# A delta-rule recurrence by chunks: the triangular matrices by products of their own, both directions in one triangle, operands stored by half stream

## The chip, the cores and the metric

The kernel runs on one core of one Trainium2 chip. The metric is device time in microseconds (us). A core has TensorE (PE, matrix products; its weight loads are shown as PEld), VectorE (DVE), ScalarE (ACT), GpSimd (POOL) and SyncE (SP), which here issues every DMA. Each engine works through its own queue in order and waits on semaphores where it needs what another has made. 

## The reference, cut to what matters

The program is a whole network of three layers over 256 tokens and 256 context tokens of 1024 features, in float32. The change lies in the second layer's mixer, a delta-rule state per head: 16 heads of 64 features, run over the tokens forwards and backwards, first over the context and from its final state over the tokens.

```python
def rwkv7_scan(r, w, k, v, a, b, state, reverse, with_out):
    def step(s, inp):
        rt, wt, kt, vt, at, bt = inp
        sa = jnp.einsum('bhij,bhj->bhi', s, at)
        s = s * wt[:, :, None, :] + sa[..., None] * bt[:, :, None, :] + vt[..., None] * kt[:, :, None, :]
        y = jnp.einsum('bhij,bhj->bhi', s, rt) if with_out else None
        return s, y
...
    yc_f, yc_b, st_f, st_b = bidir(cxt, s0, s0, need_ctx)
    yl_f, yl_b, _, _ = bidir(lat, st_f, st_b, True)
```

The kernel does it by chunks of 32 steps. With a', b', k', r' the operands with their decays, a chunk needs U = (I - tril(a' b'T, -1))^-1 (a' S + tril(a' k'T, -1) V), outputs Y = r' S + tril(r' b'T) U + tril(r' k'T) V, and a new state S. The backward direction has the other triangle.

## The kernel before, in words

**Input stage** (`rwkv_in` and what it starts; about 930 to 1054 us of the profile). Projections and low-rank products run on PE, and for each direction z and each of 8 feature tiles k `ri_item` (L2344) and `ri_decayed` (L2404) make the operands on DVE, ACT and POOL. `ri_send` (L2304) stores each to DRAM: `d_bk` (keys, 512 KB a store), `d_q` (removal keys, 256 KB), `d_rd` (receptances, 128 KB), laid out as [partition, feature tile, time], so that a store writes one run per partition.

**Recurrence** (`rwkv_scan`, L2430; about 1054 to 1357 us). It runs in four units: context first half, context second half, tokens first half, tokens second half (`UNITS`). For a unit j:

- `rw_operands` (L2510) loads, per direction, `we` (two loads of 64 partitions from `d_q`) and `bk` (one load from `d_bk`), and for token units two loads from `d_rd`. A unit is half of the tokens, so a partition's data come in 8 separate runs of 512 bytes (`d_q`, `d_rd`) or 1 KB (`d_bk`).
- `rw_inner` (L2534): 64 items (direction, feature tile, chunk). For each, two products of 64x64 give all four triangles of a chunk (L2551, L2552) in PSUM tile `pA`, two buffers. A mask on DVE (L2558, two per PSUM tile) writes them into `we`, next to the removal keys. POOL then multiplies decays into half of the keys (L2567). Context units take 16 items to a PSUM tile, token units 8, with the receptances beside.
- `rw_items` (L2570) takes the 32x32 blocks to be inverted out of `we`: four transposes of 32 partitions on DVE (L2586), one per direction and parity of the head, into `N`, with reversed axes for the backward direction; after each a POOL memset (L2588) clears the block in `we`.
- `rw_inverse` (L2593): forward substitution, one matrix per partition, all 128 at once: 30 pairs of DVE instructions (L2605, L2607). Two transposes of 64 partitions (L2615) write the inverse to `tt`.
- `rw_chain` (L2712), for two groups of heads: four steps a unit, each a removal product (L2734), a copy, a product with the inverse (L2745), four copies with a scale (L2750), a state product (L2764), two copies (L2775). Token units add outputs (L2797); the last unit a read-out (L2871).

The four inverses run one after the other, and unit j's steps need unit j's inverse.

**The order** is planned in the program: `Weave` (L294) runs all these threads as generators against engines with stated costs, and emits each engine's instructions in the order in which they would start. A cost is only the planner's: it sets places in the queues, not durations. The planner also adds products of no use on PE (`rw_warm`, L2620, into `pX`), which keep TensorE's clock up: where it sees PE idle for more than 0.25 us it fills 80% of the gap, and behind each row of an inverse it adds some where the planned work of PE falls below a share (`DUTY`, 0.5 or 0.55). Those of the second kind wait for their DVE row, and what stands behind them on PE waits too. `rw_heat` (L2630) puts 12 such products ahead of the recurrence, and 8 more that wait for the last load issued so far.

```python
        for k in range(1, 31):
            m = 31 - k
            us = 0.07 + 0.00105 * m * k
...
            row = nc.vector.tensor_tensor(N[:, k + 1 :, :k], N[:, k + 1 :, :k], pr, op=ALU.add)
            self.weave.keep(self.weave.now, 0.0, row)
```

SP's queue at the start holds unit 0's loads (forward, then backward), unit 1's removal keys, then small loads of values `uv` (L2669), each behind a POOL memset of its buffer (L2663), then the rest of unit 1 and unit 2.

Of the kernel before, what the change touches and what calls it, by code (L numbers as in the profile page):

```python
# [18 lines left out]
P = 128  # L19
# [10 lines left out]
class Stream:  # L30
    """A weight matrix as a row of [128, nb] units, loaded in tiles of WCOL
    columns and split into two float32r parts whose sum is exact."""
# [11 lines left out]
    def load(self, t):  # L44
        """a tile of the matrix on its way"""
# [34 lines left out]
class KB:  # L80
# [32 lines left out]
    def open_psum(self, **banks):  # L113
        """all of PSUM: banks per pool"""
# [4 lines left out]
    def open_gemm(self, n=4):  # L119
        """the pools of the products with weights"""  # L120
# [21 lines left out]
    def row_in(self, name, n, pool=None):  # L142
        """a row of n numbers, the same in all partitions"""
# [8 lines left out]
    def act_set(self, after, name):  # L152
        """load a named activation table right behind an instruction"""
# [5 lines left out]
    def mm3(self, ps, wh, wl, xh, xl, start, stop):  # L159
        """ps += (wh + wl).T @ (xh + xl) in three float32r passes"""  # L160
# [9 lines left out]
    def begin(self, g):  # L170
        """runs a generator's first part; the others follow behind later products"""
# [49 lines left out]
    def rstd_tok(self, sums, n, width, scale, eps):  # L221
        """(sums * scale + eps) ** -0.5 on a [128, n] tile"""
# [7 lines left out]
    def sumsq(self, pool, xs, kt):  # L230
        """for each x the sum over its feature tiles of x squared: [128, T], the partitions still to add"""
# [12 lines left out]
    def rstd_from(self, acc, n_feat):  # L244
        """token-major 1/rms [128, 2] from the squares' partial sums"""
# [5 lines left out]
    def bcast_tok(self, rs, pool, col=0, n=2):  # L251
        """rs [128 tokens, n] -> [128, n * 128], the same row in all partitions"""
# [11 lines left out]
class Phase:  # L264
    """pools of one phase: tag -> number of buffers, opened together"""
# [20 lines left out]
def bc(ap, axis, n):  # L286
    """ap with a new axis of n equal entries at free position axis"""
# [6 lines left out]
class Weave:  # L294
    """Emits threads of work, each a generator of requests, in the order in which the
# [1591 lines left out]
class Third(First):  # L1887
# [542 lines left out]
    def rwkv_scan(self):  # L2430
        nc = self.nc
        es = ExitStack()
        with es:
# [707 lines left out]
```

## Time and profile before

| | |
|---|---|
| median of 3 runs | 2858.17 us (2854.01 to 2858.56) |
| profiled execution, span from first to last instruction | 2854.8 us; the page has no other time for this execution |
| input stage of the layer, 930 to 1056 us | DVE busy 110.6 us, PE 109.3 us, DMA engines busy 0.67 of the time |
| recurrence, about 1054 to 1357 us | 303 us, 10.6% of the span |
| of it, from the first product of unit 0 to the last inverse | 1076.6 to 1298.3 us |

A busy share over the whole span says little here, since the network's other layers are products with weights; the recurrence is read by its own stretches.

### The profile page before, as it was taken

The page shows a single profiled execution, that of the slowest core. Times are in us where ns is not written, and L with a number is a line of the kernel's source. Part 1 is how long each engine was busy: PE and PEld are TensorE (multiplying, and loading weights), DVE is VectorE, ACT ScalarE, POOL GpSimd, SP SyncE. Part 2 cuts the span into 40 slices and gives each one's busy share as a digit, 9 for nine tenths or more (in the row PEclk, how much of TensorE's full clock was granted, in tenths as well). Part 3 has the DMA queues.
Part 4 walks back from the last instruction along what each step waited for, and adds up shares of the span by engine and source line. Part 5 has one row for each costly group of instructions (what it writes and reads, how often), then busy time and mean ns, then how long its engine had stood idle before and what let it go on. Part 6 is the DMA issues. An engine that isn't in the chain of part 4 may idle for free.

```text
span 2854.8 us, 52905 instructions
## 1 busy us (share of the span) xinstructions
PE 2654.0 (93%) x22052; PEld 2362.1 (83%) x22052; DVE 1763.1 (62%) x2885; ACT 1297.4 (45%) x2358; POOL 402.5 (14%) x392
## 2 busy tenths in 40 slices
PE   5999999999968879887899999999999999799999
PEld 3977567888757666765899999998999999798999
DVE  4453564334386966885774665776665665765764
ACT  3344333223245541675553544555444444655443
POOL 1210100000044552342100001011001001311100
PEclk9999989999978889998999999999999999999999
DMA  7244735223223675323455455433455554233554
GB/s 274 89 156 152 260 126 191 103 89 104 83 72 107 226 228 114 81 68 96 139 186 179 170 183 198 163 134 119 167 188 177 178 186 172 96 105 110 177 178 148
DMA packets 108142, 426.29 MB, mean 149 GB/s; under 512 B 14334, under 2 KB 50430, under 8 KB 66046
## 3 DMA queue, kind: packets, MB, share of 16 engines
q1 hardware_dynamic: 107326, 420.76, 43.1%
q8 instruction: 173, 2.83, 0.4%
q10 hardware_dynamic: 576, 2.15, 0.2%
q14 instruction: 67, 0.55, 0.1%
HBM read 397.68 MB, written 24.13 MB: 148 GB/s over the span
## 4 chain that ended last, share of the span: by engine, by line
PE 78%; DVE 13%; ACT 4%; POOL 2%; issue 2%; DMA 1%; SPq 0%; ACTq 0%; DVEq 0%; POOLq 0%
PE g L162 20%; PE g L163 20%; PE g L164 20%; PE pG L162 2%; PE pG L163 2%; PE pG L164 2%; DVE pr L2605 2%; DVE N L2607 2%; PE d L1343 2%; PE pX L2623 1%; DVE wl L72 1%; PE pA L2551 1%; POOL acc L495 1%; DVE we L2558 1%; POOL rs L227 1%
## 5 line engine op out<-in xcount | busy, mean ns | idle before, releaser
L72 DVE TENSOR_TENSOR wl<-raw,wh 128x1024 fp32r<-128x1024 f32 x512 | 626.9, 1225 | 427.7 <-ACT wh L71 425.5
L71 ACT CAST wh<-raw 128x1024 fp32r<-128x1024 f32 x512 | 535.2, 1047 | 638.0 <-PE g L163 546.2
L163 PE MATMUL g<-xnl,wh 128*128 128x256 f32 x1504 | 427.9, 285 | 1.0 <-DVE xnl L168 1.0
L162 PE MATMUL g<-xnh,wh 128*128 128x256 f32 x1504 | 427.4, 285 | 1.3 <-ACT xnh L167 1.3
L164 PE MATMUL g<-xnh,wl 128*128 128x256 f32 x1504 | 427.9, 285 | 0.0
L162 PE MATMUL g<-hh,wh 128*128 128x256 f32 (+1 forms) x1216 | 374.4, 308 | 4.9 <-ACT wh L71 3.4
L164 PE MATMUL g<-hh,wl 128*128 128x256 f32 (+1 forms) x1216 | 373.3, 307 | 0.7 <-DVE wl L72 0.7
L163 PE MATMUL g<-hl,wh 128*128 128x256 f32 (+1 forms) x1216 | 373.9, 308 | 0.0
L162 PEld LDWEIGHTS g<-xnh,wh 128*128 128x128 f32 x1504 | 290.5, 193 | 1.7 <-ACT xnh L167 1.7
L163 PEld LDWEIGHTS g<-xnl,wh 128*128 128x128 f32 x1504 | 290.6, 193 | 1.5 <-DVE xnl L168 1.5
L164 PEld LDWEIGHTS g<-xnh,wl 128*128 128x128 f32 x1504 | 290.7, 193 | 0.0
L162 PEld LDWEIGHTS g<-hh,wh 128*128 128x128 f32 x1216 | 234.6, 193 | 17.5 <-ACT wh L71 4.0
L163 PEld LDWEIGHTS g<-hl,wh 128*128 128x128 f32 x1216 | 234.3, 193 | 14.2 <-DVE hl L1382 2.5
L164 PEld LDWEIGHTS g<-hh,wl 128*128 128x128 f32 x1216 | 234.1, 193 | 12.5 <-issue 1.7
L495 POOL TENSOR_TENSOR acc<-acc,sq 128x256 f32<-128x256 f32 x63 | 65.8, 1045 | 863.5 <-ACT sq L494 381.2
L162 PE MATMUL g<-dh,wh 128*128 128x512 f32 (+1 forms) x512 | 172.0, 336 | 0.0
L163 PE MATMUL g<-dl,wh 128*128 128x512 f32 (+1 forms) x512 | 172.0, 336 | 0.0
L164 PE MATMUL g<-dh,wl 128*128 128x512 f32 (+1 forms) x512 | 172.0, 336 | 0.0
L2623 PE MATMUL pX<-ident 128*128 128x256 f32 (+3 forms) x388 | 106.9, 386 | 32.8 <-DVE N L2607 17.9
L163 PE MATMUL g<-wl,hh 128*128 128x256 f32 x448 | 128.4, 287 | 6.9 <-DVE wl L72 6.9
L162 PE MATMUL g<-wh,hh 128*128 128x256 f32 x448 | 131.2, 293 | 3.3 <-ACT wh L71 3.2
L164 PE MATMUL g<-wh,hl 128*128 128x256 f32 x448 | 127.8, 285 | 0.0
(590 smaller groups left out, 5961.7 us busy)
## 6 DMA issues: line engine op xcount, KB each, us to landing
raw<-in_w_mlp SPq DMA_DIRECT2D x64, 1024.0 KB, 4.8
raw<-in_w_ada SPq DMA_DIRECT2D x48, 1024.0 KB, 6.3
raw<-in_w_pre_gu SPq DMA_DIRECT2D x44, 1024.0 KB, 4.8
raw<-in_w_post_gu SPq DMA_DIRECT2D x44, 1024.0 KB, 4.8
raw<-in_w_pre_down SPq DMA_DIRECT2D x22, 1024.0 KB, 4.8
raw<-in_w_post_down SPq DMA_DIRECT2D x22, 1024.0 KB, 4.8
raw<-in_w_ab SPq DMA_DIRECT2D x14, 1024.0 KB, 4.9
d_bk<-h SPq DMA_DIRECT2D x16, 512.0 KB, 3.0
```

Source lines behind the costliest of these rows:

```text
L71: nc.scalar.copy(h[:, :w], r)
L72: nc.vector.tensor_tensor(l[:, :w], r, h[:, :w].bitcast(F32), op=ALU.subtract)
L162: mm(ps, wh, xh, start=start, stop=False)
L163: mm(ps, wh, xl, start=False, stop=False)
L164: mm(ps, wl, xh, start=False, stop=stop)
L227: nc.gpsimd.tensor_tensor(rs[:, :n], ms[:, :n], self.mhalf[:, :n], op=ALU.pow)
L495: nc.gpsimd.tensor_tensor(acc, acc, sq, op=ALU.add)
L1343: nc.tensor.matmul(ps[32 * j : 32 * j + 32], self.cpad[:, k0 + j, 30 - 2 * n : 62 - 2 * n], raw[:, j * 512 : (j + 1) * 512], start=n == 0 ...
L2551: nc.tensor.matmul(ps[64:, i], bk[:64, i0 + i], we[0][:64, :W, i0 + i], start=True, stop=True)
L2605: nc.vector.tensor_tensor(pr, bc(N[:, k + 1 :, k], 2, k), bc(N[:, k, :k], 1, m), op=ALU.mult)
L2607: row = nc.vector.tensor_tensor(N[:, k + 1 :, :k], N[:, k + 1 :, :k], pr, op=ALU.add)
L2623: mm = self.nc.tensor.matmul(o, self.ident, bc(self.ident[:, :64], 1, cols // 64), start=True, stop=True)
```

## The change

- The operands are stored by half stream: `d_bk`, `d_q`, `d_rd` get a leading axis of 4 or 2 halves, so a unit's load reads one run of 4 KB (`we`) or 8 KB (`bk`) per partition, and a store writes 4 (or 2) runs of 512 bytes or 1 KB per partition.
- The backward direction's removal operands are stored in reversed order within a chunk, so that both directions have one triangle; one POOL instruction more per backward tile in `ri_decayed`.
- The matrices to be inverted get products of their own (`rw_matrices`): four of 64x32 per pair of items, two PSUM tiles a unit, each masked by one DVE instruction over 128 partitions into `tt`. One transpose of 128 partitions takes them to `N`, one takes the inverse back.
- `rw_inner` no longer makes that block: products are 64x32, two per item in context units, four in token units; masks of 32 or 64 partitions, two per tile of 16 items in context units, four per tile of 8 in token units. The blocks that were cleared after each transpose are cleared once at the start (12 POOL memsets), ahead of the other POOL work.
- One thread (`rw_products`) orders them: for unit 0 forward inner products, matrices, backward inner products; for the others matrices first. The decays go into the keys after that. The chain waits for all inner products.
- The planner's costs are restated (DVE rows of the inverse 0.2 + 0.0015 m k, ACT copies 0.37, DVE read-out 0.42). `eng = yield "ACT"` still gets ACT, so the copies stay on it.

```diff
-        self.d_bk = [dt(f"d_bk{z}", [P, KT, 2 * 2 * T]) for z in range(2)]
-        self.d_q = [dt(f"d_q{z}", [P, KT, 2 * T]) for z in range(2)]
-        self.d_rd = [dt(f"d_rd{z}", [P, KT, T]) for z in range(2)]
+        self.d_bk = [dt(f"d_bk{z}", [4, P, KT, 2 * T // 2]) for z in range(2)]
+        self.d_q = [dt(f"d_q{z}", [4, P, KT, T // 2]) for z in range(2)]
+        self.d_rd = [dt(f"d_rd{z}", [2, P, KT, T // 2]) for z in range(2)]
...
-        self.nc.sync.dma_start(dst, src)
+        n = dst.shape[0]
+        self.nc.sync.dma_start(dst.rearrange("b p f -> p b f"), src.rearrange("p (b f) -> p b f", b=n))
...
-        kp, bp = bk[:, :, z], bk[:, :, 1 - z]
+        kp, bp = bk[:, :, z], rv3(bk[:, :, 1 - z])
...
+            self.on(eng).tensor_tensor(co[:, :, :, :0:-1], ck[:, :, :, :31], cE[:, :, :, 1:], op=ALU.mult)
+            yield "Pool", 0.1
+            nc.gpsimd.tensor_tensor(o[:, :, 0], kk[:, :, 31], E[:, :, 32], op=ALU.mult)
+            yield "Pool", 0.1
+            nc.gpsimd.tensor_copy(o[:, :, 32], kk[:, :, 63])
...
+            for j, u in enumerate(self.us):
+                for z in range(2):
+                    for par in range(2):
+                        r = self.row(par, 1 - z)
+                        nc.gpsimd.memset(u["we"][par][r : r + 32, 0, z * 32 : z * 32 + 32], 0.0)
...
+    def rw_products(self):
+        for j, (s, h) in enumerate(self.UNITS):
+            if j > 0:
+                yield from self.rw_matrices(j)
+            yield from self.rw_inner(j, s, 0)
+            if j == 0:
+                yield from self.rw_matrices(j)
+                yield from self.rw_keys_end(j, 0)
+            yield from self.rw_inner(j, s, 1)
...
-                    yield "PE", 0.64, 0.0 if i + 4 < per else 0.15, 0.17 * W
-                nc.tensor.matmul(ps[64:, i], bk[:64, i0 + i], we[0][:64, :W, i0 + i], start=True, stop=True)
-                nc.tensor.matmul(ps[:64, i], bk[64:, i0 + i], we[1][64:, :W, i0 + i], start=True, stop=True)
+                    yield "PE", 0.32 * W, 0.0 if i + 4 < per else 0.15, 0.17 * W
+                for second in (z, 1 - z)[:W]:
+                    for par in range(2):
+                        r, o = slice(64 * par, 64 * par + 64), self.row(par, second)
+                        w = slice(0, W) if second == z else slice(1, W)
+                        nc.tensor.matmul(ps[o : o + 32, i, w], bk[r, i0 + i, 32 * second : 32 * second + 32], we[par][r, w, i0 + i], start=True, stop=True)
...
+    def rw_matrices(self, j):
...
+        for i0 in range(0, 32, 16):
+            a = yield "take", "A"
+            ps = self.pA[a].rearrange("p (i t) -> p i t", t=32)
+            for i in range(16):
+                if i % 4 == 0:
+                    yield "PE", 0.64, 0.0 if i + 4 < 16 else 0.15, 0.17
+                for z in range(2):
+                    for par in range(2):
+                        q, r = 2 * z + par, slice(64 * par, 64 * par + 64)
+                        it = z * 32 + i0 + i
+                        nc.tensor.matmul(ps[32 * q : 32 * q + 32, i], bk[r, it, 32 * (1 - z) : 32 * (1 - z) + 32], we[par][r, 0, it], start=True, stop=True)
+            yield "DVE", 0.6
+            nc.vector.tensor_tensor(u["tt"][:, i0 : i0 + 16], ps, bc(self.nmask, 1, 16), op=ALU.mult)
...
-                yield "DVE", 1.13
-                rows = we[par][r0 : r0 + 32, 0, z * 32 : z * 32 + 32]
-                nc.vector.transpose(Nq[:, ::-1, ::-1] if z else Nq, rows.rearrange("p i t -> p t i"))
-                yield "Pool", 0.9
-                nc.gpsimd.memset(rows, 0.0)
+        yield "wait", ("matrices", j)
+        yield "DVE", 1.94
+        nc.vector.transpose(N, self.unit(j)["tt"].rearrange("p i t -> p t i"))
...
-            us = 0.07 + 0.00105 * m * k
+            us = 0.2 + 0.0015 * m * k
...
-        for z in range(2):
-            r = slice(64 * z, 64 * z + 64)
-            yield "DVE", 1.13
-            row = nc.vector.transpose(tt[r].rearrange("p i t -> p t i"), N[r, ::-1, ::-1] if z else N[r])
+        yield "DVE", 1.94
+        row = nc.vector.transpose(tt.rearrange("p i t -> p t i"), N)
```

## Rows read from the trace of the kernel before

**Rows 1.** The page: span, and the chain that ended last by line.
```profile
span 2854.8 us, 52905 instructions
PE g L162 20%; PE g L163 20%; PE g L164 20%; PE pG L162 2%; PE pG L163 2%; PE pG L164 2%; DVE pr L2605 2%; DVE N L2607 2%; PE d L1343 2%; PE pX L2623 1%; DVE wl L72 1%; PE pA L2551 1%; POOL acc L495 1%; DVE we L2558 1%; POOL rs L227 1%
```
**Rows 2.** Busy time by stretch: window, its length, engines with counts, clock, DMA share, GB/s.
```profile
930.00:1056.00 126.00, 109.30 (x607) 84.15 (x606) 110.56 (x130) 69.34 (x108) 74.85 (x79) 0.89 0.67 228
1060.00:1076.00 16.00, 8.86 (x28) 7.01 (x27) 0.00 (x0) 0.00 (x0) 0.00 (x0) 0.68 1.01 227
1136.40:1186.80 50.40, 44.37 (x1068) 36.87 (x1056) 45.33 (x82) 35.60 (x88) 13.25 (x20) 0.95 0.17 43
1186.80:1241.40 54.60, 48.24 (x1109) 39.73 (x1108) 45.53 (x82) 33.84 (x84) 21.09 (x28) 0.94 0.38 92
1241.40:1298.30 56.90, 43.68 (x1112) 35.90 (x1112) 51.16 (x70) 35.82 (x91) 29.21 (x32) 0.86 0.31 71
1298.30:1357.00 58.70, 45.78 (x1208) 36.12 (x1207) 28.64 (x74) 36.52 (x88) 14.25 (x15) 0.95 0.34 109
```
**Rows 3.** Groups of instructions from 1136.4 to 1298.3 us, units 1 to 3.
```profile
L2623 PE MATMUL pX<-ident 128*128 128x64 f32 (+3 forms) x183 | 44.4, 345 | 19.3 <-DVE N L2607 14.2 <-DVE tt L2615 5.0
...
L2558 DVE TENSOR_TENSOR we<-pA,amask 64x512 f32<-64x512 f32 x36 | 24.6, 688 | 13.3 <-PE pA L2552 12.4
```
**Rows 4.** PE in order of time, up to the first inner product.
```profile
1070.11 6.58 PE L2623 MATMUL pX<-ident 128*128 128x256 f32 x16 [7.14 <-DMA we<-d_q]
1076.62 0.24 PE L2551 MATMUL pA<-we,bk 64*64 64x32 f32 x1
```
**Rows 5.** DVE in order of time, around the first inverse.
```profile
1091.78 1.41 DVE L2558 TENSOR_TENSOR we<-pA,amask 64x512 f32<-64x512 f32 x2 [5.89 <-PE pA L2552]
1093.21 1.94 DVE L2586 STREAM_TRANSPOSE N<-we 32x1024 f32<-32x1024 f32 x1
...
1105.44 1.94 DVE L2586 STREAM_TRANSPOSE N<-we 32x1024 f32<-32x1024 f32 x1
1107.42 0.20 DVE L2605 TENSOR_TENSOR pr<-N 128x30 f32<-128x30 f32 x1
...
1132.49 3.90 DVE L2615 STREAM_TRANSPOSE tt<-N 64x1024 f32<-64x1024 f32 x2
```
**Rows 6.** Groups of instructions in the whole recurrence, shapes apart.
```profile
L2586 DVE STREAM_TRANSPOSE N<-we 32x1024 f32<-32x1024 f32 x16 | 31.0, 1939 | 0.5
L2615 DVE STREAM_TRANSPOSE tt<-N 64x1024 f32<-64x1024 f32 x8 | 15.4, 1924 | 0.2
L2588 POOL MEMSET we<- 32x1024 f32 x16 | 15.1, 944 | 47.8 <-DVE N L2586 44.4 <-PE pU L2745 2.4 <-DMA we<-d_q 0.9
L2879 DVE TENSOR_TENSOR we<-pY,we 128x256 f32<-128x256 f32 x8 | 3.3, 417 | 11.9 <-PE pY L2797 11.9
```
**Rows 7.** PE in order of time: products among the first inner products, and the first chain step.
```profile
1081.95 0.70 PE L2623 MATMUL pX<-ident 128*128 128x256 f32 x2
1082.58 0.24 PE L2551 MATMUL pA<-we,bk 64*64 64x32 f32 x1
1083.16 0.70 PE L2623 MATMUL pX<-ident 128*128 128x256 f32 x2
...
1137.15 0.65 PE L2745 MATMUL pU<-wsb,tt 32*32 32x64 f32 x32
1137.73 0.92 PE L2623 MATMUL pX<-ident 128*128 128x256 f32 x4
```
**Rows 8.** DMA issues: KB each, us from issue to landing (page; recurrence; input stage).
```profile
raw<-in_w_mlp SPq DMA_DIRECT2D x64, 1024.0 KB, 4.8
...
bk<-d_bk SPq DMA_DIRECT2D x6, 1024.0 KB, 9.0
we<-d_q SPq DMA_DIRECT2D x12, 256.0 KB, 9.7
...
d_bk<-h SPq DMA_DIRECT2D x16, 512.0 KB, 3.0
```

More of the change, by code (lines that the diff above doesn't have):

```diff
@@ L2568, in rw_inner @@
             yield "set", ("keys", j, z, q)
+    def rw_matrices(self, j):
+        nc = self.nc
+        u = self.unit(j)
+        we, bk = u["we"], u["bk"]
+        for z in range(2):
+            yield "wait", ("operands", j, z)
+        for i0 in range(0, 32, 16):
[4 more added lines that the diff above has]
+                    yield "PE", 0.64, 0.0 if i + 4 < 16 else 0.15, 0.17
+                for z in range(2):
+                    for par in range(2):
+                        q, r = 2 * z + par, slice(64 * par, 64 * par + 64)
[3 more added lines that the diff above has]
+            nc.vector.tensor_tensor(u["tt"][:, i0 : i0 + 16], ps, bc(self.nmask, 1, 16), op=ALU.mult)
+            yield "give", ("A", a)
+        yield "set", ("matrices", j)
     def rw_items(self, j):
         nc = self.nc
[L2573 removed]
+        N = self.Ns[j % 2]
         if j > 1:
             yield "wait", ("inv", j - 2)
[L2576 to L2588 removed]
+        yield "wait", ("matrices", j)
+        yield "DVE", 1.94
+        nc.vector.transpose(N, self.unit(j)["tt"].rearrange("p i t -> p t i"))
         yield "Pool", 0.15
@@ L2608, in rw_inverse @@
             self.weave.keep(self.weave.now, 0.0, row)
-        if j > 2:
-            for g in range(2):
-                yield "wait", ("chain", j - 3, g)
-        for z in range(2):
-            r = slice(64 * z, 64 * z + 64)
-            yield "DVE", 1.13
-            row = nc.vector.transpose(tt[r].rearrange("p i t -> p t i"), N[r, ::-1, ::-1] if z else N[r])
-            if z == 0:
-                self.weave.keep(self.weave.now, 0.0, row)
+        yield "DVE", 1.94
+        row = nc.vector.transpose(tt.rearrange("p i t -> p t i"), N)
+        self.weave.keep(self.weave.now, 0.0, row)
         yield "set", ("inv", j)
@@ L2638, in rw_heat, with copy @@
                 self.rw_warm(256, after)
+    def copy(self, eng, o, i):
+        (self.nc.scalar.copy if eng == "ACT" else self.nc.vector.tensor_copy)(o, i)
     def chunk(self, z, i):
@@ L2718, in rw_chain @@
             yield "wait", ("inv", j)
+            per = 16 // (2 - s)
+            for end in range(per, 65, per):
+                yield "wait", ("inner", j, end)
             self.weave.DUTY = self.DUTIES[1 + (j == len(self.UNITS) - 1)]
@@ L2744, in rw_chain @@
                             u0 = self.row(par, 1 - z)
-                            nc.tensor.matmul(pu[u0 : u0 + 32, z, k], tt[r, item(0, k) if z == 0 else item(1, k) - 32], w[r, k * 64 : k * 64 + 64], start=True, stop=True)
+                            nc.tensor.matmul(pu[u0 : u0 + 32, z, k], tt[r, item(z, k) - 32 * z], w[r, k * 64 : k * 64 + 64], start=True, stop=True)
                 for z in range(2):
@@ L2801, in rw_output @@
             return
-        yield "ACT", 0.27
+        yield "ACT", 0.37
         nc.scalar.copy(ys, yp)
@@ L2868, in rw_pools @@
             self.wo.fill(KT)
-            yield "DVE", 1.13
+            yield "DVE", 1.94
     def rw_readout(self, g, m, yp):
@@ L2906, in rw_readout @@
         pv = pt.rearrange("p k (z t) -> p k z t", z=2)
-        yield "ACT", 0.27
+        yield "ACT", 0.37
         nc.scalar.copy(at(self.ch), pv)
-        yield "DVE", 0.35
+        yield "DVE", 0.42
         nc.vector.tensor_tensor(at(self.cl), pv, at(self.ch).bitcast(F32), op=ALU.subtract)
```

104 lines of the change are left out of this document (59 added, 45 removed).

## The prediction

> **What bounds the kernel now.** I read the page first: most of the chain that ended last is weight products of other layers; the recurrence shows as inverse rows (L2605, L2607), products of no use (L2623), inner products and masks [rows 1]. So the change can only act in about 303 us, and there the busy time by stretch decides. From the end of the first inverse to the end of the last, 1136.4 to 1298.3 us, DVE is busy 45.33 + 45.53 + 51.16 = 142.0 of 161.9 us, PE 44.37 + 48.24 + 43.68 = 136.3, ACT less; behind it, without inverses, DVE needs half of its time [rows 2]. The groups of that stretch then say who waits for whom: PE's products of no use stood idle for 19.3 us, for DVE rows 14.2 and for the transposes back 5.0 [rows 3]. DVE sets the pace there, with PE close behind. The view in order of time shows the head: PE waits 7.14 us for a load of removal keys, spends 6.58 us on the eight products tied to it, and starts inner products at 1076.62 [rows 4]; the first inverse starts at 1107.42, 30.8 us later, behind masks and four transposes, and runs 25.1 us plus 3.9 us of transposes [rows 5].
>
> **The change, step by step.** The sum stands against the span of 2854.8 us [rows 1]; the median of the runs is 3.4 us above it, and I apply the difference to the median, 2858.2.
>
> 1. *Stores in shorter runs.* 16 stores each of 512, 256 and 128 KB (14.7 MB) are cut to runs of 512 bytes and 1 KB. The input stage moves 228 GB/s at a DMA share of 0.67, some 340 GB/s when all engines work; loads in runs of that short length gave 227 GB/s at a share of 1.01 [rows 2]. So the stores take about 65 us of all engines in place of 43, and the share rises to some 0.85 of 126 us. They lie beside DVE, busy 110.6 of 126 us [rows 2]; the cover is thinner, and a buffer may come free late. SP's issue of a store in four runs costs more, beside that work too. The extra POOL instruction on each of 8 backward tiles is small and shares POOL's slack (74.85 of 126 us busy). I take +2 us: bounds 0 (all hidden) and +6 (a quarter of the 22 us shows). A gain is excluded: nothing here gets shorter.
> 2. *Loads in longer runs.* A 1 MB load of `bk` lands after 9.0 us, one of 256 KB in the same queue after 9.7, a 1 MB weight load in long runs after 4.8 [rows 8]. PE waits 7.14 us for such a load [rows 4]. I take -4: bounds 0 and -7.1, the whole wait. The 12 memsets of 0.944 us [rows 6], 11.3 us, stand ahead of the `uv` memsets on POOL, so the small loads of `uv` and what is behind them on SP (unit 1's keys) may wait a few us; unit 1 is not needed until the first inverse runs. I cost that at nothing; without that cover it is at most 11.3 us of unit 1's start.
> 3. *From the first inner product to the first inverse.* Today PE takes four items of inner products and two products of no use every 1.21 us, 0.63 of it the latter [rows 7]; 16 such groups stand ahead of the last mask, then transposes [rows 5]. Afterwards 8 groups of forward inner products, whose planned PE time is halved (I take 0.8 us: 0.58 and some filler), then 8 groups of matrices. Such a group has 16 products, 32 records; 32 records of 32x32 took 0.58 us [rows 7], with filler 1.21. 8 x 0.8 + 8 x 1.21 = 16.1, one mask 0.69, one transpose 1.94 (32 and 64 partitions cost the same, 1.94 and 1.92 [rows 6], so 128 should), waits 1: 20 us in place of 30.8, -11. Bounds: -8 (all groups at 1.21) and -19 (no filler). The row gives 18 ns a record.
>    The Trainium skill (TensorE: Matmul & The Clock Gate, "Wait — 56ns, not 53.3ns?") says that matmuls never start less than about 25 ns apart however small they are. By that a group of matrices would take 0.8 us, an estimate, and step 3 would be -9; the row shows 18 ns, and the row decides.
> 4. *The first inverse.* One transpose back instead of two: -1.9. But other DVE work now stands among its rows: four backward masks (2.75), unit 1's two matrix masks (1.4), its transpose (1.94) and, as PE delivers them, four of its masks (2.75): +8.8. Net +7. Bounds +1 (only the backward masks) and +12.
> 5. *Units 1 to 3, DVE.* Transposes out: 12 of 1.94 become 2 (unit 1's is in step 4), -19.4. Transposes back: 6 of 1.92 become 3, -5.8. Masks: 36 of 0.688 (24.8 [rows 3]) become 4 of unit 1, 4 of matrices, and 64 of 256 columns, for which the nearest row is 0.417 [rows 6]: 2.8 + 2.8 + 26.7 = 32.3, +7.5. Net -17.7 of 142.0, and with the idle 19.9 us kept, 144 in place of 161.9. The 16 POOL memsets [rows 6] leave too; no engine but POOL and its own successors waited on them, so nothing.
> 6. *The same stretch, PE.* Matrices of units 2 and 3: 16 groups of 0.58 us, +9.3; token units' inner products go from two to four per item, but a group of four items then has 32 records, 0.58 us by the 32x32 row, where a group of 16 larger ones took 0.58 in a context unit [rows 7] (I take the same for token units): +2, for what a change of shape may cost. PE's list becomes about 148 us with 44.4 us of filler in it [rows 2, 3]; of its 25.6 idle us, 19.3 are waits for DVE that shrink. So PE allows no better than 148 to 154. I take 148, -14: between DVE's 144 and PE's 154, nearer to DVE, since real products displace some filler. Bounds -28 (idle halved too, filler down) and 0.
> 7. *The last unit* (58.7 us [rows 2]): its chain is untouched, 0.
>
> Sum: +2 - 4 - 11 + 7 - 14 = -20, so 2838 us.
>
> **The rivals.** *DVE stays filled and filler gives way* (gain larger): half of the 19.9 idle us vanish and PE drops as much filler; step 6 becomes -28 and the sum -34, 2824 us. For it: waits for PE by masks (12.4 us [rows 3]) shrink when products come earlier. Against: PE's list.
> *PE becomes the bound*: step 6 is -4 rather than -14, the sum -10, 2848 us. For it: PE is busy 136.3 of 161.9 already [rows 2]. The Trainium skill's 25 ns of step 3, if it held for these products, would lead here: 48 groups of 32 records in the stretch at 0.8 us in place of 0.58, +10.6, an estimate; the row speaks against it.
> *Slower, by the planner's own filler.* The restated costs make a planned inverse 26.9 us of row time instead of 14.6 (the sums of both formulas over 30 pairs); the rows really took 25.1 [rows 5]. PE gaps in the plan are filled, and a planned stretch that is 12.3 us longer per inverse may be filled to 80%: 3 x 9.8 = 29.5 us more products in PE's own queue, which no engine can skip. PE's list is then 148 + 29.5 = 177.5, +15.6 on the stretch in place of -14: the sum is +9.6, 2868 us. It decides from the point where filler in the stretch exceeds the 44.4 us of now by about 20. For it: PE's queue is in order. Against: the same longer plan ends the waits of PE for rows (14.2 us), and masks that the plan now sets among the rows use up planned time.
> *The change gives nothing* (within 6 us): loads gain nothing, since the weight load's 4.8 us was measured with nothing else in its queue, and steps 4 and 6 eat step 3. Around 2857.
>    Of the loads, the Trainium skill (DMA: Bandwidth & Descriptors, Specifications) puts the least transfer for full rate at 512 bytes. By it neither the shorter stores nor the longer loads change a rate, steps 1 and 2 are 0 and the sum is -18; the row with 227 GB/s at full share speaks against it [rows 2].
>
> **How the numbers follow.** The forecast (2828 to 2844) gets 0.50, the larger gain 0.20, PE as the bound 0.13, nothing 0.09, slower 0.08. About 0.2%, 5.7 us, is what a measurement of this kernel can tell from no change: faster 0.83, same 0.09, slower 0.08. The range takes in the forecast, most of the larger gain and PE as the bound with the ends of steps 1 to 4: 2815 to 2854.
>
> **What would show it.** Right: the first L2605 row some 15 us sooner after the input stage than now, one transpose of about 1.94 us on each side of every inverse, DVE busy near 125 us between the first and last inverse, that stretch near 148 us, the last stage unchanged. Step 2: the wait of PE for a load under 4 us. Step 1 is wrong if the input stage ends over 6 us later. The forecast is wrong if a transpose of 128 partitions costs more than 1.94, if masks of 256 columns cost 0.688 as those of 512 (then +17 us on DVE, and the gain is gone), or if the products of no use exceed 44.4 us by 20 in the stretch.

## The result and the profile after

The changed kernel takes **2885.8 us** (median of 4 runs, 2883.4 to 2886.9), where the kernel before took 2856.1 beside it: ratio 1.0102, 95% interval 1.0088 to 1.0116. It is 29 us slower by the ratio; the forecast was 20 us faster, and the range ended at 2854. The page of the changed kernel, span and chain that ended last by line (compare [rows 1]):

```profile
span 2885.1 us, 56428 instructions
PE g L162 19%; PE g L163 19%; PE g L164 19%; PE pX L2675 3%; PE pG L162 2%; PE pG L163 2%; PE pG L164 2%; PE d L1343 2%; PE pS L2826 1%; DVE wl L72 1%; POOL acc L495 1%; DVE N L2665 1%; PE pA L2589 1%; POOL rs L227 1%; DVE pr L2663 1%
```

Products of no use (L2675, before L2623) rise from 1% to 3% of the chain, and the inverse's rows fall from 4% to 2%. The chain has moved from DVE's rows to PE's products. The busy time by stretch says where (columns as in [rows 2]):

```profile
930.00:1058.00 128.00, 113.25 (x609) 87.78 (x608) 110.95 (x130) 70.24 (x108) 75.28 (x81) 0.86 0.71 227
1130.00:1160.50 30.50, 28.24 (x664) 23.01 (x668) 28.28 (x63) 22.66 (x56) 7.84 (x11) 1.00 0.09 24
1160.50:1206.70 46.20, 41.61 (x1078) 33.55 (x1072) 8.08 (x10) 26.66 (x67) 9.21 (x14) 0.93 0.42 111
1206.70:1252.50 45.80, 39.91 (x1054) 31.37 (x1041) 38.48 (x93) 17.89 (x43) 11.26 (x15) 0.96 0.36 76
1252.50:1277.20 24.70, 24.34 (x780) 19.61 (x783) 3.31 (x3) 19.25 (x51) 22.16 (x23) 1.00 0.11 26
1277.20:1323.40 46.20, 42.29 (x1116) 33.36 (x1109) 39.14 (x94) 18.84 (x47) 12.06 (x17) 0.93 0.26 82
1323.40:1388.00 64.60, 54.84 (x1232) 45.45 (x1233) 32.16 (x83) 38.31 (x96) 11.07 (x12) 0.97 0.20 62
```

Inverses are called here by their unit: first inverse for unit 0, then inverse 1, 2 and 3, which is the last. The first inverse ends at 1130.0, 6.4 us sooner than in [rows 2]. From there to the end of the last one 193.4 us pass, against 161.9. DVE does less (28.28 + 8.08 + 38.48 + 3.31 + 39.14 = 117.3 us, against 142.0), so its idle time goes from 19.9 to 76.1 us. Nearly all of the growth lies in the third and the fifth line: 46.2 us with 8.1 us of DVE work, 24.7 with 3.3. DVE in order of time shows the first hole, from the end of inverse 1 to the start of inverse 2:

```profile
1158.52 1.95 DVE L2668 STREAM_TRANSPOSE tt<-N 128x1024 f32<-128x1024 f32 x1
1160.50 2.00 DVE L2598 TENSOR_TENSOR we<-pA,amask 32x512 f32<-32x512 f32 x3
1171.18 1.41 DVE L2598 TENSOR_TENSOR we<-pA,amask 32x512 f32<-32x512 f32 x2 [8.68 <-PE pA L2589]
1174.85 1.41 DVE L2598 TENSOR_TENSOR we<-pA,amask 32x512 f32<-32x512 f32 x2 [2.26 <-PE pA L2589]
1191.60 0.69 DVE L2634 TENSOR_TENSOR tt<-pA,nmask 128x512 f32<-128x512 f32 x1 [15.35 <-PE pA L2632]
1203.96 0.69 DVE L2634 TENSOR_TENSOR tt<-pA,nmask 128x512 f32<-128x512 f32 x1 [11.67 <-PE pA L2632]
1204.69 1.97 DVE L2646 STREAM_TRANSPOSE N<-tt 128x1024 f32<-128x1024 f32 x1
```

Read it upwards. Inverse 2 waits for the masks of unit 2's matrices (L2634), these for PE's products (L2632, 15.35 and 11.67 us). The matrices stand in `rw_products` behind unit 1's inner products, whose last masks (L2598) run at 1160 to 1176, behind inverse 1. In the kernel before, with the same lag on unit 1's masks (`MASK`), they could not slide so far: the blocks to be inverted came out of those masks, so inverse 1's transposes waited for them. DVE there, behind the first inverse:

```profile
1136.42 2.60 DVE L2558 TENSOR_TENSOR we<-pA,amask 64x512 f32<-64x512 f32 x4
1139.05 1.93 DVE L2586 STREAM_TRANSPOSE N<-we 32x1024 f32<-32x1024 f32 x1
```

After the change inverse 1 asks for unit 1's matrices alone, and seven of unit 1's eight masks run behind it. What PE does in that hole, its groups from 1160.5 to 1204.7 us:

```profile
L2675 PE MATMUL pX<-ident 128*128 128x256 f32 (+3 forms) x68 | 17.2, 359 | 0.0
L2826 PE MATMUL pS<-uv,bki 128*64 128x64 f32 x192 | 7.7, 240 | 0.2 <-ACT uv L2693 0.2
...
L2632 PE MATMUL pA<-we,bk 64*32 64x32 f32 x256 | 4.5, 207 | 3.3 <-issue 3.3
```

A count behind x is of the profile's records, and a product of this kernel leaves two of them: the 20 products of `rw_heat` are 40 records. Below, products of no use are counted in records; the x2 of [rows 7] is one product, where the prediction says two.

4.5 us of matrices share the hole with 17.2 us of products of no use and six state products of the chain. In the second hole, from inverse 2's end to the start of inverse 3, PE is busy 22.43 of 22.80 us, 8.9 of them with products of no use (the stretch, with PE, clock, DMA share and GB/s, and one of its groups):

```profile
1252.50:1275.30 22.80, 22.43 (x700) 1.00 0.09 22
L2675 PE MATMUL pX<-ident 128*128 128x256 f32 (+2 forms) x36 | 8.9, 342 | 0.0
```

In the whole stretch from 1130.0 to 1323.4 us the products of no use take 82.5 us, where [rows 3] has 44.4:

```profile
L2675 PE MATMUL pX<-ident 128*128 128x256 f32 (+3 forms) x334 | 82.5, 360 | 9.8 <-DVE N L2665 8.3 <-DVE tt L2668 1.2
```

The last stage is nearly as before: from the end of the last inverse to the end of the read-out (1384.5, before 1357.7) 61.1 us, before 59.4.

### The profile page after: what moved, and what is told of

Same layout as the page of the kernel before. It is cut to its first block, busy times and chain, and to the rows that moved or that the text cites. A ratio compares the mean times of both kernels' runs of the same rounds, so it can differ in the third digit from the quotient of the medians.

```text
span 2885.1 us, 56428 instructions
## 1 busy us (share of the span) xinstructions
PE 2698.6 (94%) x23794; PEld 2402.9 (83%) x23794; DVE 1732.0 (60%) x2909; ACT 1297.2 (45%) x2358; POOL 402.5 (14%) x396
## 4 chain that ended last, share of the span: by engine, by line
PE 79%; DVE 10%; ACT 4%; issue 2%; POOL 2%; DMA 1%; SPq 0%; ACTq 0%; DVEq 0%; POOLq 0%
PE g L162 19%; PE g L163 19%; PE g L164 19%; PE pX L2675 3%; PE pG L162 2%; PE pG L163 2%; PE pG L164 2%; PE d L1343 2%; PE pS L2826 1%; DVE wl L72 1%; POOL acc L495 1%; DVE N L2665 1%; PE pA L2589 1%; POOL rs L227 1%; DVE pr L2663 1%
## 5 line engine op out<-in xcount | busy, mean ns | idle before, releaser
L2675 PE MATMUL pX<-ident 128*128 128x256 f32 (+3 forms) x594 | 148.3, 373 | 18.1 <-DVE N L2665 10.3
L2675 PEld LDWEIGHTS pX<-ident 128*128 128x128 f32 x594 | 102.8, 203 | 38.5 <-DVE N L2665 15.0
```

Source lines behind the costliest of these rows:

```text
L2675: mm = self.nc.tensor.matmul(o, self.ident, bc(self.ident[:, :64], 1, cols // 64), start=True, stop=True)
```

## The experiments

**Theories.** A: unit 1's masks let rows go first (`MASK`, 0.2 us for unit 1) and hold both PSUM tiles `pA` meanwhile, so unit 2's matrices, next in the thread, come only after inverse 1. B: products of no use make PE late. C: the restated costs spoil the planned order. D: the storage costs the time. The expectations call the products that the duty asks for "tied to rows"; more exactly, duty 0 takes away those behind a row and those that the planner puts ahead of a product where the planned share falls short, and leaves those that fill gaps.

**The storage alone, on the kernel before (e1).**

```diff
-        self.d_bk = [dt(f"d_bk{z}", [P, KT, 2 * 2 * T]) for z in range(2)]
+        self.d_bk = [dt(f"d_bk{z}", [4, P, KT, 2 * T // 2]) for z in range(2)]
...
-        load(u["bk"][:, it], self.d_bk[z][:, :, 2 * tk.start : 2 * tk.stop])
+        load(u["bk"][:, it], self.d_bk[z][2 * s + b])
```

(and `d_q`, `d_rd`, `ri_send` as in the change.)

> The kernel before with the storage by half stream alone (stores in 2 or 4 runs per partition, loads in one run). Steps 1 and 2 of the prediction together are -2 us, so about 2854 us. Theory A (the products' order makes inverses 2 and 3 start late): 2850 to 2860 us, first inner product within 4 us of 1076.6. A rival that puts the loss into the input stage and the loads (short stores, contention): 2870 us or more, the input stage ending over 6 us later.

Measured: 0.9994 of before (0.9981 to 1.0007). D falls. The first inner product was not within 4 us of 1076.6 in the profiled execution, the slowest of its ten (2864.8 us): it started at 1081.4, behind a longer wait for a load than before (7.14 in [rows 4]):

```profile
1074.86 6.63 PE L2624 MATMUL pX<-ident 128*128 128x256 f32 x16 [9.39 <-DMA we<-d_q]
```

**Masks at once (e2).**

```diff
-    MASK = 0.0, 0.2, 0.0, 0.0
+    MASK = 0.0, 0.0, 0.0, 0.0
```

> The changed kernel, but unit 1's masks no longer let the inverse's rows go first (lag 0 in place of 0.2 us). Theory A (the masks of unit 1 hold both PSUM tiles of the products, so unit 2's matrices, behind them in the same thread, come after inverse 1): unit 2's matrices are done before inverse 1 ends, inverse 2 begins under 8 us behind inverse 1 in place of 46 us, and the time falls by 15 to 40 us, to 2845 to 2870 us, even though masks now stand among inverse 1's rows. Theory B (the planner's products of no use lengthen PE's queue): their number stays near 600, so 2880 to 2890 us. Theory C (the restated costs): no change, 2880 to 2890 us.

Measured: 1.0032 of before (1.0012 to 1.0052), so 20 us under the changed kernel's 1.0102, with 530 records of products of no use in place of 594. DVE in order of time, at the place of the hole:

```profile
1182.88 1.94 DVE L2668 STREAM_TRANSPOSE tt<-N 128x1024 f32<-128x1024 f32 x1
1184.85 1.73 DVE L2598 TENSOR_TENSOR we<-pA,amask 32x256 f32<-32x256 f32 x4
1186.50 1.97 DVE L2646 STREAM_TRANSPOSE N<-tt 128x1024 f32<-128x1024 f32 x1
```

Inverse 2 begins 1.7 us behind inverse 1, its matrices being masked from 1137.9 on, before inverse 1 began. The masks now lie among the rows: the first inverse ends at 1142.2, 12 us later than in the changed kernel, 3.3 of it because the first inner product started later in this execution. The second hole shrinks too, from 22.8 to 8.9 us. A holds.

**No products of no use (e3), and the same on the kernel before (e5).**

```diff
-            w.BIAS, w.AGING = 0.02, 0.1
+            w.BIAS, w.AGING, w.FILL = 0.02, 0.1, 0.0
...
-    DUTIES = 0.5, 0.55, 0.5
+    DUTIES = 0.0, 0.0, 0.0
```

> The changed kernel without the products of no use in the recurrence (duty 0 and gaps left open; the 20 of heat ahead of it stay). Theory B: the idle stretches of DVE of 46 and 25 us between the inverses shrink to under 15 us each, and the time falls to 2840 to 2860 us, unless the granted clock falls to its lower level for most of the recurrence. Theory A: unit 2's matrices still come only behind unit 1's masks, so inverse 2 still begins 30 us or more behind inverse 1; the time moves by less than 12 us at the same clock, 2874 to 2895 us.

> The kernel before without the products of no use in the recurrence (duty 0, gaps left open; the 20 of heat stay): the control to the same edit on the changed kernel, which took 25 us off it. Theory B' (products of no use cost the changed kernel time that they do not cost the kernel before, since only there PE stands in the way of the next unit's matrices): before moves by less than 12 us, 2846 to 2870 us. Rival (products of no use cost any version of this recurrence some 25 us): 2828 to 2840 us.

Measured: e3 1.0015 of before (1.0001 to 1.0028), 25 us under the changed kernel, though the granted clock was 0.61 up to the end of the first inverse. The hole ahead of inverse 2 is still 29 us (1154.4 to 1183.7), as A says; the one ahead of inverse 3 is gone (1.1 us), as B says. Neither expectation alone was right. e5: 1.0038 (1.0022 to 1.0054), 11 us slower: there the products of no use are worth their place. The granted clock was 0.57 from 1060 to 1140 us, close to the lower of its two levels (1.2 of 2.4 GHz), with PE busy 38.25 of 80 us:

```profile
1060.00:1140.00 80.00, 38.25 (x614) 33.48 (x612) 48.11 (x85) 6.61 (x18) 20.65 (x26) 0.57 0.60 135
```

**The old costs (e4), and the new costs on the kernel before (e9).**

```diff
-            us = 0.2 + 0.0015 * m * k
+            us = 0.07 + 0.00105 * m * k
...
-                        eng = yield "ACT", 0.37, 0.0
+                        eng = yield "ACT", 0.27, 0.0
```

(and so at each of the other restated lines; e9 is the reverse.)

> The changed kernel with the planner's costs of before (rows of an inverse 0.07 + 0.00105 m k, ACT copies 0.27, DVE read-out 0.35); no instruction is other, only the order and the number of the products of no use. Theory C: the loss goes, 2835 to 2860 us. Theory A: the lag of unit 1's masks stays, inverse 2 begins 25 us or more behind inverse 1, and the time falls by no more than 12 us, 2874 to 2888 us. Theory B: the planned inverse is 12 us shorter each, so 100 or more fewer products of no use and 2850 to 2870 us.

> The kernel before with the restated costs of the planner alone (rows of an inverse 0.2 + 0.0015 m k, ACT copies 0.37, DVE read-out 0.42): the prediction's third rival taken by itself. That rival, with its terms: some 30 us more of products of no use in the stretch, +15 to +25 us, 2870 to 2885 us. Theory A with B (the loss needs the new products' thread, in whose way the filler stands): more filler, but the next unit's triangles come with its inner products early, so within 10 us of before, 2850 to 2868 us.

Measured: e4 1.0113 (1.0097 to 1.0129), no gain; inverse 2 begins 46.6 us behind inverse 1, and 544 records of products of no use are left, so B's way to a gain did not open. In e4's stretch between first and last inverse (1128.7 to 1327.8 us) they take as long as in the changed kernel, with the old costs:

```profile
L2675 PE MATMUL pX<-ident 128*128 128x64 f32 (+3 forms) x322 | 82.1, 364 | 14.0 <-DVE N L2665 12.5 <-issue 0.8 <-DVE tt L2668 0.3
```

So the restated costs are not what makes the changed kernel slow, and C falls. e9: 1.0046 (1.0031 to 1.0060), 13 us slower, between the two expected effects (15 to 25, and under 10); products of no use in the stretch between first and last inverse rise from 44.4 [rows 3] to 63.0 us, and the stretch from 161.9 to 174.4 us. So the prediction's third rival exists on the kernel before, at about half of its price.

**Both edits (e6).** The diffs of e2 and e3 together:

```diff
-            w.BIAS, w.AGING = 0.02, 0.1
+            w.BIAS, w.AGING, w.FILL = 0.02, 0.1, 0.0
...
-    DUTIES = 0.5, 0.55, 0.5
+    DUTIES = 0.0, 0.0, 0.0
...
-    MASK = 0.0, 0.2, 0.0, 0.0
+    MASK = 0.0, 0.0, 0.0, 0.0
```

> The changed kernel with unit 1's masks at once (lag 0) and without products of no use: both edits together. If they act on two different waits (A on the order of the products' thread, B on the length of PE's queue), their gains of 20 and 25 us add up: 2835 to 2850 us, with no idle of DVE over 10 us between inverses. If they are two ways to the same place (unit 2's matrices come sooner), no more than the larger: 2855 to 2870 us.

Measured: **0.9927 of before (0.9898 to 0.9956)**, 2841.8 us: better than both kernels, and 44 us under the changed one by the medians, 50 by the ratios, so the gains of 20 and 25 add up. Stretches up to the end of the first inverse, to that of the last, and behind it:

```profile
1060.00:1139.80 79.80, 41.34 (x1396) 35.34 (x1395) 40.22 (x85) 6.61 (x18) 31.34 (x41) 0.65 0.53 141
1139.80:1284.70 144.90, 102.89 (x3836) 85.04 (x3836) 119.97 (x253) 105.38 (x262) 52.86 (x68) 0.92 0.30 78
1284.70:1345.00 60.30, 38.98 (x1124) 32.80 (x1124) 28.78 (x74) 36.47 (x86) 14.75 (x16) 0.75 0.33 105
```

144.9 us between first and last inverse with DVE busy 120.0: the forecast had 148 and about 125.

**Which products of no use cost (e10, e13, e14).** Duty 0 with gaps still filled, with masks at once (e10) and without (e13); and gaps open with the duty kept (e14):

```diff
-    DUTIES = 0.5, 0.55, 0.5
+    DUTIES = 0.0, 0.0, 0.0
```

e10 has this and the diff of e2, e13 this alone, and e14:

```diff
-            w.BIAS, w.AGING = 0.02, 0.1
+            w.BIAS, w.AGING, w.FILL = 0.02, 0.1, 0.0
```

> The changed kernel with masks at once and duty 0, but gaps in PE's plan filled as in the kernels before and after (so only the products that wait for a row of an inverse are gone). If it is the products tied to rows that cost time in the changed kernel: as without any, 2835 to 2848 us, or 3 to 8 us better by a granted clock near 0.96 in place of 0.61 to 0.95. If any product of no use in PE's queue costs: between 2850 and 2868 us.

> The changed kernel without the products of no use that are tied to rows (duty 0), gaps filled as before, lag of unit 1's masks kept. If the tied kind costs the 25 us by the order that it makes: 2855 to 2868 us, as without any. If it is the mere time of products of no use in PE's queue: their gap kind still costs, 2870 to 2885 us.

> The changed kernel without the products that fill gaps, those tied to rows kept; the planned order is that of the changed kernel. If the tied kind and its order cost the 25 us: within 6 us of the changed kernel, 2880 to 2892 us. If the time of the gap kind in PE's queue costs: 2862 to 2876 us.

Measured: e10 0.9935 (0.9910 to 0.9960), e13 1.0013 (0.9999 to 1.0028): each as the run without any (e6, e3), though e10 has 260 and e13 288 records of these products against 40. What fills a gap of PE costs nothing that these runs can tell (the intervals of e13 and e3 leave room for some 5 us, those of e10 and e6 for some 10), and the clock that it gives back (0.76 in place of 0.65 up to the first inverse's end in e10) gains nothing that can be measured. e14: 1.0102 (1.0079 to 1.0124), as the changed kernel. It tells less than was meant, since the duty asks for most of what the gaps had (570 records are left of 594). So it is the duty that costs 25 us (e13 against the changed kernel). PE's groups in the same hole of e13, 1158.5 to 1189.9 us:

```profile
L2675 PE MATMUL pX<-ident 128*128 128x256 f32 (+3 forms) x28 | 7.4, 393 | 0.0
L2826 PE MATMUL pS<-uv,bki 128*64 128x64 f32 x114 | 5.0, 250 | 0.2 <-ACT uv L2693 0.2
...
L2632 PE MATMUL pA<-we,bk 64*32 64x32 f32 x256 | 3.5, 212 | 0.0
```

The hole is 31.4 us in place of 44.2: 9.8 us less of products of no use and 78 records less of state products stand between the same 256 records of the matrices. In neither hole do products of no use wait for anything (idle 0.0), and no inverse runs there, so here it is their place ahead of the matrices that costs, not a row that they are tied to. The second hole goes from 22.8 to 1.1 us with the duty, but inverses 2 and 3 take longer (53 and 50 us from transpose to transpose, 44 each in the changed kernel): the stretch between first and last inverse is 173.7 us in e13, 193.4 in the changed kernel.

**The restated costs without the duty (e15, and its control e16).** On the kernel before, duty 0 with gaps filled; e15 has the new costs too:

```diff
-    DUTIES = 0.5, 0.55, 0.5
+    DUTIES = 0.0, 0.0, 0.0
```

And in e15 alone, with the other restated lines:

```diff
-            us = 0.07 + 0.00105 * m * k
+            us = 0.2 + 0.0015 * m * k
```

> The kernel before with the restated costs and without the tied kind. If the restated costs act through the tied kind (a longer planned inverse asks for more of it): the 13 us that they cost alone are gone, no slower than the kernel before with the tied kind left out (e16), within 6 us. If they act by the places that they give to rows and masks: 10 us or more slower than e16.

> The kernel before without the tied kind, gaps filled: the control to e15, and to the 11 us that leaving out both kinds costs the kernel before. If that loss comes from the lower granted clock (0.57 ahead of the first inverse): filled gaps give it back, 2856 to 2866 us. If it comes from the order that is planned without the tied kind: 2868 to 2878 us again.

Measured: e16 1.0025 (1.0010 to 1.0040), e15 0.9969 (0.9954 to 0.9984). The same costs that lose 13 us with the duty gain 16 without it. On the kernel before they cost time through the duty, then, and apart from that they make the better plan. e16 is 4 us under e5, within both intervals; its filled gaps raised the granted clock up to the first inverse's end only from 0.57 to 0.64, so how much of e5's loss is the clock and how much the order stays open.

**Other versions (e7, e8, e11, e12, e17, e18).** All have masks at once. e8 and e17 give the matrices of units 1 to 3 a thread of their own, and take them out of `rw_products`:

```diff
             w.add(self.rw_products(), 1)
+            w.add(self.rw_mats(), 1)
...
+    def rw_mats(self):
+        yield "wait", ("matrices", 0)
+        for j in range(1, len(self.UNITS)):
+            yield from self.rw_matrices(j)
```

They and e18 have duty 0 and gaps open, as e6; e8 and e18 have the costs of e4. e7 has the costs of e4, filled gaps and a duty of 0.3:

```diff
-    DUTIES = 0.5, 0.55, 0.5
+    DUTIES = 0.3, 0.3, 0.3
```

e11 and e12 have gaps open and a duty of 0.2, and e12 the old cost of rows and a lower one of matrices:

```diff
-    DUTIES = 0.5, 0.55, 0.5
+    DUTIES = 0.2, 0.2, 0.2
...
-                    yield "PE", 0.64, 0.0 if i + 4 < 16 else 0.15, 0.17
+                    yield "PE", 0.4, 0.0 if i + 4 < 16 else 0.15, 0.17
...
-            us = 0.2 + 0.0015 * m * k
+            us = 0.07 + 0.00105 * m * k
```

> The changed kernel with unit 1's masks at once, the planner's costs of before and a duty of 0.3 in place of 0.5 and 0.55 (fewer products of no use, gaps still filled). By A and B together: unit 2's matrices before inverse 1 ends, under 350 products of no use, 2825 to 2850 us. If the restated costs matter beside them (C, in part), it is under 2835 us; if old costs only make the order worse, as alone, 2855 to 2875 us.

> The changed kernel with the matrices of units 1 to 3 in a thread of their own, so that they no longer stand behind a unit's inner products, unit 1's masks at once, old costs, no products of no use. Theory A, if the one thread matters beside the lag: the matrices of units 2 and 3 are done before the inverse ahead ends, DVE is idle under 5 us between inverses, 2820 to 2845 us. If the lag alone mattered: as the same without the thread, within 6 us of 2845 us.

> The same with duty 0.2 and no filled gaps: fewer than 100 products of no use. If the lower clock in the first inverse (0.61 without filler) costs what the longer first inverse suggests, 5 to 10 us come back: 2830 to 2838 us. If not, 2836 to 2848 us, as without any.

> The changed kernel with masks at once, duty 0.2, no filled gaps, the cost of the rows alone as before (0.07 + 0.00105 m k) and the matrices' products planned at 0.4 us a group of four in place of 0.64, near what the trace shows (0.39). If what is left is the order of the products against the rows (masks among the rows of the first inverses, unit 3's matrices late): under 2835 us, inverses 1 to 3 within 140 us of the first one's end. If the rows' restated cost is the better one: 2840 to 2860 us.

> As e6 (masks at once, no products of no use, restated costs), with the matrices of units 1 to 3 in a thread of their own. If the one thread costs something beside the lag: 2825 to 2838 us, under e6. If it was the thread that made e8 slow: 2850 to 2866 us. If neither: within 6 us of e6, 2836 to 2848 us.

> As e6, with the costs of before in place of the restated ones, one thread. If the old costs made e8 slow: 2855 to 2868 us. If they do not matter without tied products: within 6 us of e6, 2836 to 2848 us.

| run | ratio to before | 95% interval |
|---|---|---|
| e7 | 0.9939 | 0.9921 to 0.9956 |
| e8 | 0.9994 | 0.9981 to 1.0008 |
| e11 | 0.9958 | 0.9943 to 0.9973 |
| e12 | 0.9988 | 0.9976 to 0.9999 |
| e17 | 0.9968 | 0.9956 to 0.9980 |
| e18 | 1.0004 | 0.9990 to 1.0017 |

The own thread gains nothing (e17 against e6, e8 against e18): of theory A the lag stands; without the lag the one thread costs nothing, and an own thread with the lag kept was not run. The old costs lose without duty (e18 against e6, 22 us), as in e15 and e16. e11 gives nothing for its 112 records of products of no use: it is 9 us over e6, with intervals that overlap, and outside both of its expected ranges. e7 fits no rule found here: old costs with a duty of 0.3 and filled gaps are as good as e6, although e18 is not. A planned order can differ in many places for one setting; the runs settle the two edits, not a law of the duty.

## Why the prediction was wrong

**Steps 1 and 2 came out near their sum by luck.** In the two traces the store of `d_cf`, near the input stage's end, is issued 2.7 us later (1056.3, before 1053.6; said +2), and PE waited less for the keys:

```profile
1069.89 5.27 PE L2675 MATMUL pX<-ident 128*128 128x256 f32 x16 [5.30 <-DMA we<-d_q]
1075.09 1.46 PE L2589 MATMUL pA<-we,bk 64*32 64x32 f32 x80
```

First inner product at 1075.1 in place of 1076.6: -1.5, said -2. But these times differ from one execution to the next by more than that. That store is issued at 1053.0 to 1058.4 us in the five traces with the storage of before (before, e5, e9, e15, e16) and at 1052.3 to 1058.1 in the fifteen with the new one, so step 1's loss can't be seen; the DMA share was 0.71, not 0.85. The wait is 7.1 to 8.9 us in those five traces and 4.6 to 9.4 in the fifteen: about 1 us less in the mean, not 4, and nowhere under 4. In 12 us from about 2 to 3 us behind the first load's issue, the DMA share was 1.12 to 1.14 in four traces with the old storage and 0.97 to 1.03 in five with the new, but the rate nearly the same, 250 to 264 GB/s and 255 to 288. With e1's ratio, a sum with both steps at nothing fits as well.

**Step 3 was right, its gain 14.3 us where 11 was said.** DVE around the first inverse:

```profile
1083.22 0.69 DVE L2634 TENSOR_TENSOR tt<-pA,nmask 128x512 f32<-128x512 f32 x1 [2.40 <-PE pA L2632]
1088.82 0.69 DVE L2634 TENSOR_TENSOR tt<-pA,nmask 128x512 f32<-128x512 f32 x1 [4.91 <-PE pA L2632]
1089.55 1.97 DVE L2646 STREAM_TRANSPOSE N<-tt 128x1024 f32<-128x1024 f32 x1
1091.55 0.21 DVE L2663 TENSOR_TENSOR pr<-N 128x30 f32<-128x30 f32 x1
...
1128.07 1.92 DVE L2668 STREAM_TRANSPOSE tt<-N 128x1024 f32<-128x1024 f32 x1
```

16.5 us from the first product to the first row, said 20 (before 30.8). A group of 32 records of matrices held PE for 0.39 us up to the next group (below), 12 ns a record, where the forecast's row gave 0.58 and 18:

```profile
1180.68 0.46 PE L2632 MATMUL pA<-we,bk 64*32 64x32 f32 x32
1181.07 0.66 PE L2748 MATMUL pT<-ident,bk 128*128 128x128 f32 x4
```

Inside this group the records start in fours, 6 to 7 ns apart, one for each of four parts of the array, and from one four to the next 32 ns pass.

The Trainium skill (TensorE: Matmul & The Clock Gate, "Wait — 56ns, not 53.3ns?") gives a least distance of about 25 ns between starts; this trace does not agree, with its 6 to 7 ns, for products of 64x32 that fall in different parts of the array.

**Step 4 was near in size, but not for its reasons.** From the first row to the end of the transpose back 38.5 us pass, before 29.0: +9.5, said +7. DVE's work there grew by 1.6 us only (28.4, before 26.8). Of what the step counted, the four backward masks and unit 1's two matrix masks came; unit 1's transpose and masks did not, as its masks let the rows go first. The rest is waiting, which the step had at nothing: 1.6 us for inner products, and 6.3 for unit 1's matrices, the wait that was to sink step 5 (us in total, times, longest, from 1091.55 to 1130.0 us):

```profile
DVE tt L2634 <- PE pA L2632: 6.3, 1, 6.3
```

From the first inner product to the first inverse's end 54.9 us pass, before 59.8: -4.9, where steps 3 and 4 had said -4.

**Step 5 failed, at "with the idle 19.9 us kept".** The removed and added work was priced well: masks and transposes (the groups of the recurrence below) are as forecast, but for 4.7 us of unit 1's that step 4 had counted and that fell behind the first inverse. Busy time was 117.3 us (said 124.3), since the rows of the last inverse took 24.6 us in place of 36.8, for a reason that the last section gives. But the idle time became 76.1 us:

```profile
L2598 DVE TENSOR_TENSOR we<-pA,amask 64x256 f32<-64x256 f32 x32 | 13.5, 422 | 1.0
L2598 DVE TENSOR_TENSOR we<-pA,amask 32x256 f32<-32x256 f32 x32 | 13.4, 420 | 10.0 <-PE pA L2589 9.2
L2668 DVE STREAM_TRANSPOSE tt<-N 128x1024 f32<-128x1024 f32 x4 | 7.8, 1950 | 0.1
L2634 DVE TENSOR_TENSOR tt<-pA,nmask 128x512 f32<-128x512 f32 x8 | 5.5, 691 | 62.1 <-PE pA L2632 62.0
```

The last line holds the miss: eight masks of 0.69 us, and 62.0 us in which DVE waited for the products ahead of them. Of these 48.4 us lie behind the first inverse, as the waits from 1130.0 to 1323.4 us say (us in total, times, longest):

```profile
DVE tt L2634 <- PE pA L2632: 48.4, 4, 15.3
```
An idle time may be kept only if the order that makes it is kept. Before, the blocks to be inverted came out of the masked inner products, so unit 1's masks, lag or not, were done ahead of inverse 1, and unit 2's products could follow during it (the first of their masks at 1146.95). Afterwards inverse 1 does not need those masks, and unit 2's matrices stand behind them, in the same thread and for the same two PSUM tiles; the prediction never followed that thread past unit 1. e2 takes the lag away: the first hole is gone, 20 us back.

**Step 6 failed with it.** PE's list was said to be 148 us with 44.4 of products of no use; it was 28.24 + 41.61 + 39.91 + 24.34 + 42.29 = 176.4 with 82.5. The products that count took 93.9 us of it, some 2 more than before, where +11.3 was said. The deciding point of the **slower rival**, 20 us above 44.4, was passed, and its PE list of 177.5 us was met, but by accident: it laid the products of no use to the restated costs, and e4, with the old costs, has 82.1 us of them in a list of 177.4. What the runs show in its place: products of no use that fill gaps cost nothing that can be told (e10, e13), those that the duty asks for cost 25 us, and the lag costs 20 to 25 more, with them (e2) or without (e3 against e6). The rival was priced from three planned inverses at 80% of filled gaps; the kind that counted was the other one, from the duty, which the kernel's account names only in part (those behind a row, and not those ahead of a product) and the prediction left out of its sum. Why the duty asks for some 82 us in this kernel with either costs was not taken apart. A chance of 0.08 for slower was far too low for a kernel in which costs, order and threads all changed at once.

**Step 7** held within 2 us.

e6 comes out at the forecast's figures: a stretch of 144.9 us (said 148) and 2841.8 us (said 2838). It gets there in part by another way, without the 44.4 us of products of no use, and with no gain up to the first inverse's end (60.0 us from the first inner product, before 59.8). The prediction priced DVE's work and took the order for granted.

## What to carry to other kernels

Where a planner sets the order, a change that moves work into another thread has to be followed through that thread for every round, with the buffers that it takes and who gives them back: the busy time of the engine that sets the pace says what can be gained, and the idle time is not a constant. When stated costs are corrected, look at every rule that works on the planned time; on the kernel before, the restated costs lose 13 us with the duty and gain 16 without it. Of the products that keep the clock up, those that filled gaps of the plan cost nothing that these runs can tell, and those that a share asked for, ahead of products that DVE waited for, cost 25 us.

## What the hardware showed that was not expected

DVE's rows of an inverse slow down beside GpSimd. The same row, 128x30 at the end of an inverse, takes 0.19 us in the changed kernel's first inverse and 2.36 us in e6's last one; both engines there in order of time, DVE first:

```profile
1277.69 1.31 DVE L2665 TENSOR_TENSOR N<-N,pr 128x58 f32<-128x58 f32 x1
1279.03 1.28 DVE L2663 TENSOR_TENSOR pr<-N 128x30 f32<-128x30 f32 x1
1280.34 2.36 DVE L2665 TENSOR_TENSOR N<-N,pr 128x30 f32<-128x30 f32 x1
```

```profile
1277.66 2.60 POOL L2905 TENSOR_TENSOR we<-we 128x512 f32<-128x512 f32 x2
1280.22 0.61 POOL L2764 TENSOR_TENSOR bki<-ident,ends 64x256 f32<-64x256 f32 x1
1280.80 1.26 POOL L2905 TENSOR_TENSOR we<-we 128x512 f32<-128x512 f32 x1
1282.02 0.61 POOL L2764 TENSOR_TENSOR bki<-ident,ends 64x256 f32<-64x256 f32 x1
```

Each row lasts about as long as the POOL instructions that it meets (1.31 and 1.28 beside POOL's of 1.30, 2.36 beside 0.61, 1.26 and 0.61). All 42 rows of the changed kernel that took over 0.15 us more than the shortest of their kind overlap a POOL product, 44 of 44 in the kernel before and 48 of 48 in e6. Masks, which read one of their two inputs from PSUM, are not slowed: 17 of the changed kernel's 80 overlap a POOL product, and none took over 0.70 us. The 60 rows of the last inverse sum to 36.8 us before, 36.9 in e6 and 24.6 in the changed kernel, where POOL's products of the read-out (L2905) ran from 1249 to 1274 us, nearly all in the second hole. So up to 12 us of e6's stretch may be there to be had, an estimate from these sums; that was not tried. The Trainium skill (SBUF — State Buffer, "SBUF: two separate sides") says that GpSimd and a DVE operation with two SBUF inputs share a port pair that one of them holds for a whole instruction while the other blocks; the trace agrees. A transpose of 128 partitions costs what one of 32 does (1.95 us against 1.94 in [rows 6]), as forecast.
